# Opening loads reordered in a two-layer hybrid token mixer, with early modulation weights in other buffers

## The chip, the cores and the metric

One core of a Trainium2 chip runs the whole program. The metric is the device time of one execution in microseconds (us). TensorE (PE) multiplies matrices, VectorE (DVE), ScalarE (ACT) and GpSimd (POOL) work on tiles, SyncE (SP) issues most DMAs. An engine executes its instructions in the order in which they were put on it; the engines wait for one another through semaphores.

## The reference, cut to what matters

Two layers work on two streams of 256 tokens each, width 1024: stream 0 is the context, stream 1 the latent. What the change touches is the head of the first layer: modulation vectors from `c` and `c_ctx`, the modulated norm of both streams, and the first input projection (the low-rank latents `mla_cq`, `mla_ckv`, `mla_kr` and `gla_glr`, 448 columns in all).

```python
shift, scale, gate = jnp.split(jax.nn.silu(c) @ ada_w[l] + ada_b[l], 3, axis=-1)
shift_c, scale_c, gate_c = jnp.split(jax.nn.silu(c_ctx) @ ada_w[l] + ada_b[l], 3, axis=-1)
h = rms_norm(x, pre_g[l]) * (1.0 + scale[:, None]) + shift[:, None]
hc = rms_norm(cx, pre_g[l]) * (1.0 + scale_c) + shift_c
...
cq = rms_norm(in_proj(hh, w_in, 'mla_cq'), q_norm)
```

Behind that each layer runs four mixers (latent attention, neighbourhood attention, long convolution, gated linear attention), gates and merges them, and projects the sum; all of that is the same in both kernels.

## The kernel before, in words

Everything is f32; a product is made of three matmuls, because each operand is split into a high part (a rounded copy, made on ScalarE) and a low part (the difference, made on VectorE). Weights come as `raw` tiles of 448 or 512 KB (`piece`, L422, three buffers) and leave as pairs `wh`, `wl` from a pool of eight each.

Work is written as generators. `spawn` (L300) enters a task, `drive` (L308) keeps a clock that advances by estimated matmul costs and lets the task of best priority that is ready run its next piece; the pauses come from the table `WAIT` (L207) and, for the first modulation, from `ADA_AT` (L204). What comes out of this is TensorE's order, which is fixed. The other engines and the DMA queue get their order from a scheduler that works on the written program.

The head of the program, in `main` (L1516): rows of x go to four tiles `x0` (512 KB each; two for stream 0, two for stream 1), then come the modulation weights of layer 0 for scale and shift. They are eight pieces of 1 MB: quarter `j` of the channels (0 to 3) times `part` (shift, scale), each loaded by `ada_load` (L543) in two halves. Quarters 0 and 1 go to `wh`/`wl` buffers (all 16 of them), quarter 2 to the pool `s`, quarter 3 to the four `x0` buffers once these are free. Between them stand the four pieces of the latent weights (`w_latent`, 448 KB each).

`ada_first` (L582) takes the eight pieces in turn: 16 small matmuls into a PSUM tile `ada`, a copy of it (`rows`) by VectorE, four matmuls that turn it by 90 degrees (`adat`, in `ada_sum` L559), and an addition into `ab`, the scale and shift per channel. `norm_in` (L629), one task per stream, squares the rows on ScalarE, gets the reciprocal root on GpSimd (`rstd`), scales on VectorE (`xn`), turns them on TensorE in four quarters (`ht`), applies scale and shift (`h`, one half on VectorE, then the other on ScalarE) and splits the result into `hh` and `hl`. `ht` and `adat` share two PSUM buffers (pool `pt`). `latent_in` (L879) multiplies: per block of 128 tokens and quarter six matmuls `pa`. Quarter q of it wants `ab` of quarter q and the q-th piece of latent weights.

`filters` (L711) makes the long convolution's filters beside this; its tiles `w3h`, `w3l` come from the pool `gy` (tags `gh`, `gl`, four each), and GpSimd clears part of `w3l`. `setup_rest` loads small tables.

Of the kernel before, what the change touches and what calls it, by code (L numbers as in the profile page):

```python
# [9 lines left out]
F32 = mybir.dt.float32  # L10
# [6 lines left out]
P = 128  # L17
# [108 lines left out]
def _layout(x, c, ctx, c_ctx, ada_w, ada_b, pre_g, post_g, w_in, mla_q_norm, mla_w_uq, mla_kv_norm, mla_w_ukv, na_rpb,  # L126
# [74 lines left out]
PI_C3 = float(np.float32(TWO_PI - PI_C1 - PI_C2))  # L201
PI_MAX = 3.1415925
MAGIC = 12582912.0
ADA_AT = (6.0, 8.0, 6.0, 11.0, 15.0, 17.0, 17.5, 19.5)  # L204


WAIT = {  # L207
    "ada_sum": (1.34, 0),
    "ada_load": (7.75, 9.57),
    "ada_gap": (4.19, 8.22),  # L210
# [47 lines left out]
    "merged": (4.6, 3.55),  # L258
    "merged_step": (0.48, 0),
    "merged_out": (1.6, 1.24),  # L260
    "norm_first": (2.15, 8.0),
}


# [5 lines left out]
class Block:  # L270
# [63 lines left out]
    def wait(self, name):  # L334
        return WAIT[name][self.l]

# [245 lines left out]
    def ada_first(self, pieces):  # L582
        for j in range(4):
            yield 0
            for part in range(2):
                yield max(0.0, ADA_AT[2 * j + part] - self.clock)
                ps = self.ps(self.pa, "ada")
                for half in range(2):
                    self.ada_mm(half, pieces[j, part, half], ps, half == 0, half == 1)
                rows = self.ada_rows(part)  # L590
                self.nc.vector.tensor_copy(rows, ps[:, 0:256])
                yield self.wait("ada_sum")
                self.ada_sum(0, part, j, rows)
            self.abq[0] = j + 1
# [818 lines left out]
    def layer(self, l, ws):  # L1413
# [12 lines left out]
        else:  # L1426
            halves = {c: self.rows(self.w_latent(l, (2 * c, 2 * c + 1))) for c in (1, 0)}
            ws = halves.get
        for g in ((0, 1),) if l == 0 else ((1,), (0,)):
            a = self.spawn(self.latent_in(l, ws, g, outs, lats), 0)  # L1430
            if g[0] in outs:
                yield lambda: a.done
# [83 lines left out]
    def main(self):  # L1516
        nc, d = self.nc, self.d
        self.setup()
        self.h, self.ht, self.hq, self.abq, self.aq = {}, {}, [0, 0], [0, 0], 0
        loaded = [self.filter_mlp(0)]  # L1520
        self.load_first()
        pieces = {}

        def ada(j, alloc):
            for part in range(2):
                for half in range(2):
                    pieces[j, part, half] = self.ada_load(0, part, j, half, alloc(half))

        early = lambda half: [self.wp.tile([P, 512], F32, tag=("wh", "wl")[half], name=self.name("adaw")) for _ in range(2)]
        xt = {}  # L1530
        for s in range(2):
            for j in range(2):
                xt[s, j] = self.M("x0")
                nc.sync.dma_start(xt[s, j], d["xin"][2 * s : 2 * s + 2, :, j * 512 : j * 512 + 512].rearrange("t p n -> p t n"))
        ada(0, early)
        ada(1, early)
        first = self.w_latent(0, (0, 1))
        ada(2, lambda half: [self.S("adaw"), self.S("adaw")])
        first += self.w_latent(0, (2, 3))
        ada(3, lambda half: [self.M("adaw").rearrange("p a b -> p (a b)")])  # L1540
        loaded += [self.window(self.S), self.filter_in(0, 0)]
        nc.sync.dma_start(self.dft, d["dft"])
        loaded.append(self.filter_in(0, 1))

        def later():
            yield from self.ada_first(pieces)
            self.setup_rest()

        self.spawn(later(), 0)
        for s in range(2):  # L1550
            self.spawn(self.norm_in(0, s, [xt[s, 0], xt[s, 1]]), 0)
        self.filt_task = self.spawn(self.filters(0, loaded), 1)

        def layers():
            for l in range(DEPTH):
                yield from self.layer(l, first if l == 0 else None)

        self.spawn(layers(), 5)
        with self.tc.manual_schedule(engines={mybir.EngineType.PE}):
            self.drive()  # L1560
# [19 lines left out]
```

## Time and profile before

| | |
|---|---|
| median of 3 runs | 1393.2 us (1391.38 to 1393.54) |
| the profiled execution | 1392.82 us |
| its span, first to last instruction | 1391.0 us |
| TensorE busy | 1310.1 us, 94% of the span |
| VectorE, ScalarE, GpSimd busy | 901.3, 603.4, 320.2 us |
| read from HBM | 163.45 MB, 122 GB/s over the span |

Times below are counted from the span's start. A busy engine is one with an instruction in it; matmuls overlap, so a busy TensorE need not be at its peak. Idle time of an engine stands in brackets with what ended it.

### The profile page before, as it was taken

The numbers are of one execution on the slowest core, as the hardware profiler recorded it, in microseconds if no ns is written. First come the engines' busy times: TensorE is split into PE (matmuls) and PEld (weight loads), VectorE is DVE, ScalarE is ACT, GpSimd is POOL, SyncE is SP. The second block draws the span as 40 slices with busy tenths as digits, with TensorE's granted clock in tenths as the row PEclk, the third lists the DMA queues.
The fourth block names the chain that finished last, engine by engine and source line by source line (L and its number), as shares of the span: only waits on it lengthen the run. The fifth ranks groups of instructions, "written<-read, shape, count | busy, mean of one in ns | idle before, by whom it ended". The sixth has DMA issues, their size and how long they took to land.

```text
span 1391.0 us, 20163 instructions
## 1 busy us (share of the span) xinstructions
PE 1310.1 (94%) x7444; PEld 1033.3 (74%) x7444; DVE 901.3 (65%) x1676; ACT 603.4 (43%) x1268; POOL 320.2 (23%) x408
## 2 busy tenths in 40 slices
PE   5899999989999999999999999979996999999996
PEld 3767677767777687666767777778775889788875
DVE  4678754676443446656565687977577787768764
ACT  4455553432322233222244454465556456445452
POOL 2232201233320201113301122442113431122110
PEclk9999999999999999999999999999998999999999
DMA  9521213232233433332422353433152366535362
GB/s 342 184 91 53 100 46 101 91 118 91 93 121 137 137 106 117 113 119 93 144 84 90 105 153 110 147 100 116 34 163 88 103 198 211 165 95 181 107 206 67
DMA packets 55506, 171.07 MB, mean 123 GB/s; under 512 B 7470, under 2 KB 10128, under 8 KB 55408
## 3 DMA queue, kind: packets, MB, share of 16 engines
q1 hardware_dynamic: 49056, 153.31, 33.4%
q0 software_dynamic: 5440, 16.16, 3.6%
q8 instruction: 59, 0.97, 0.3%
q10 hardware_dynamic: 912, 0.31, 0.1%
q14 instruction: 39, 0.32, 0.1%
HBM read 163.45 MB, written 6.31 MB: 122 GB/s over the span
## 4 chain that ended last, share of the span: by engine, by line
PE 40%; DVE 7%; issue 3%; ACT 3%; DMA 2%; POOL 1%; DVEq 0%; POOLq 0%; ACTq 0%
PE pc L386 11%; PE pj L386 10%; PE br L386 5%; PE wo L386 3%; PE sc L386 2%; PE y L386 2%; DVE wl L376 2%; PE pt L400 2%; DMA raw<-in_w_out 1%; PE pa L386 1%; ACT wh L435 1%; PE yc L386 1%; DMA raw<-in_w_in 1%; DVE ub L370 0%; PE go L386 0%
## 5 line engine op out<-in xcount | busy, mean ns | idle before, releaser
L376 DVE TENSOR_TENSOR wl<-raw,wh 128x512 fp32r<-128x512 f32 (+1 forms) x416 | 305.5, 756 | 178.2 <-ACT wh L435 171.4
L435 ACT CAST wh<-raw 128x512 fp32r<-128x512 f32 (+1 forms) x416 | 248.9, 618 | 279.9 <-DMA raw<-in_w_in 145.3
L386 PE MATMUL pc<-hh,wh 128*128 128x256 f32 (+1 forms) x688 | 242.4, 352 | 7.4 <-DVE cv L379 3.4
L386 PE MATMUL pc<-hl,wh 128*128 128x256 f32 (+1 forms) x688 | 231.5, 337 | 0.0
L386 PE MATMUL pc<-hh,wl 128*128 128x256 f32 (+1 forms) x688 | 231.3, 336 | 0.0
L386 PE MATMUL pj<-wh,hh 128*128 128x512 f32 x512 | 212.8, 416 | 3.1 <-DVE zg L379 1.6
L386 PE MATMUL pj<-wl,hh 128*128 128x512 f32 x512 | 200.2, 391 | 0.4 <-DVE wl L376 0.4
L386 PE MATMUL pj<-wh,hl 128*128 128x512 f32 x512 | 200.2, 391 | 0.0
L386 PEld LDWEIGHTS pc<-hh,wh 128*128 128x128 f32 x688 | 132.2, 192 | 32.8 <-issue 15.0
L386 PEld LDWEIGHTS pc<-hl,wh 128*128 128x128 f32 x688 | 132.2, 192 | 14.3 <-issue 2.6
L386 PEld LDWEIGHTS pc<-hh,wl 128*128 128x128 f32 x688 | 132.0, 192 | 13.7
L386 PEld LDWEIGHTS pj<-wh,hh 128*128 128x128 f32 x512 | 96.2, 188 | 33.3 <-issue 12.0
L386 PEld LDWEIGHTS pj<-wh,hl 128*128 128x128 f32 x512 | 96.1, 188 | 21.1
L386 PEld LDWEIGHTS pj<-wl,hh 128*128 128x128 f32 x512 | 96.5, 188 | 20.2 <-issue 2.6
L376 POOL TENSOR_TENSOR gl<-y,gh 128x256 fp32r<-128x256 f32 (+1 forms) x44 | 36.2, 830 | 293.5 <-ACT gh L418 293.5
L822 ACT ACTIVATE p<-sc,mx 128x512 f32<-128x512 f32 (+1 forms) x96 | 59.0, 616 | 59.3 <-DVE mx L820 56.0
L386 PE MATMUL br<-wh,gh 128*128 128x512 f32 x192 | 79.1, 412 | 5.0 <-DVE merged L379 2.6
L386 PE MATMUL br<-wl,gh 128*128 128x512 f32 x192 | 76.7, 399 | 0.0
L386 PE MATMUL br<-wh,gl 128*128 128x512 f32 x192 | 76.4, 398 | 0.0
L1336 ACT ACTIVATE gt<-pj 128x512 f32<-128x512 f32 x48 | 28.6, 596 | 90.0 <-PE pj L386 87.5
L820 DVE TENSOR_REDUCE mx<-sc 128x1 f32<-128x512 f32 (+1 forms) x96 | 55.1, 592 | 11.4 <-PE sc L386 10.5
L837 ACT COPY pt<-pt 128x256 f32<-128x256 f32 x96 | 34.2, 373 | 43.1 <-PE pt L400 42.1
(287 smaller groups left out, 2223.6 us busy)
## 6 DMA issues: line engine op xcount, KB each, us to landing
raw<-in_w_in SPq DMA_DIRECT2D x160, 512.0 KB, 3.6
adaw<-in_ada_w SPq DMA_DIRECT2D x36, 512.0 KB, 3.6
raw<-in_w_branch SPq DMA_DIRECT2D x32, 512.0 KB, 3.6
raw<-in_w_out SPq DMA_DIRECT2D x16, 512.0 KB, 4.3
adaw<-in_ada_w SPq DMA_DIRECT2D x24, 256.0 KB, 6.1
H<-filt POOLq DMA_DIRECT2D x16, 256.0 KB, 4.0
nab<-in_na_bias POOLq DMA_DIRECT2D x16, 256.0 KB, 3.0
raw<-in_w_in SPq DMA_DIRECT2D x8, 448.0 KB, 4.9
```

The source lines that it names most:

```text
L376: eng.tensor_tensor(out=out, in0=a, in1=b, op=ALU.subtract)
L386: self.nc.tensor.matmul(out, lhsT, rhs, start=start, stop=stop, skip_group_check=skip)
L400: self.nc.tensor.transpose(out, in_, self.ident)
L435: nc.scalar.copy(hi, raw[:, sl])
L820: nc.vector.tensor_reduce(out=mx, in_=ps[h][:, :nk], axis=AX.X, op=ALU.max, negate=True)
L822: nc.scalar.activation(p[h][:, :nk], ps[h][:, :nk], AF.Exp, bias=mx, scale=1.0, accum_out=sm)
L837: nc.scalar.copy(pts[h][b // 2], pp[:, b : b + 2, :])
L1336: self.nc.scalar.activation(gates[s, t], ps, AF.Tanh, scale=0.5)
```

## The change

The order of the opening loads becomes: rows of stream 1, quarter 0 of the modulation weights, two pieces of latent weights, rows of stream 0, quarters 1 and 2, the other two latent pieces, quarter 3. Quarter 0 goes to the pool `gt`, quarter 1 to the pool `gy`, so that `wh`/`wl` hold none of it. The norm of stream 1 is entered before that of stream 0, `latent_in` takes stream 1 first, and `norm_first` is longer. The table `ADA_AT` moves into `WAIT` with the same numbers.

```diff
@@ -201,10 +201,14 @@
 PI_C3 = float(np.float32(TWO_PI - PI_C1 - PI_C2))
 PI_MAX = 3.1415925
 MAGIC = 12582912.0
-ADA_AT = (6.0, 8.0, 6.0, 11.0, 15.0, 17.0, 17.5, 19.5)
+
 
 
 WAIT = {
+    "ada_at0": (6.0, 8.0),
+    "ada_at1": (6.0, 11.0),
+    "ada_at2": (15.0, 17.0),
+    "ada_at3": (17.5, 19.5),
     "ada_sum": (1.34, 0),
     "ada_load": (7.75, 9.57),
     "ada_gap": (4.19, 8.22),
@@ -258,7 +262,7 @@
     "merged": (4.6, 3.55),
     "merged_step": (0.48, 0),
     "merged_out": (1.6, 1.24),
-    "norm_first": (2.15, 8.0),
+    "norm_first": (3.27, 8.0),
 }
 
 
@@ -583,7 +587,7 @@
         for j in range(4):
             yield 0
             for part in range(2):
-                yield max(0.0, ADA_AT[2 * j + part] - self.clock)
+                yield max(0.0, WAIT[f"ada_at{j}"][part] - self.clock)
                 ps = self.ps(self.pa, "ada")
                 for half in range(2):
                     self.ada_mm(half, pieces[j, part, half], ps, half == 0, half == 1)
@@ -1426,7 +1430,7 @@
         else:
             halves = {c: self.rows(self.w_latent(l, (2 * c, 2 * c + 1))) for c in (1, 0)}
             ws = halves.get
-        for g in ((0, 1),) if l == 0 else ((1,), (0,)):
+        for g in ((1, 0),) if l == 0 else ((1,), (0,)):
             a = self.spawn(self.latent_in(l, ws, g, outs, lats), 0)
             if g[0] in outs:
                 yield lambda: a.done
@@ -1526,15 +1530,18 @@
                 for half in range(2):
                     pieces[j, part, half] = self.ada_load(0, part, j, half, alloc(half))
 
-        early = lambda half: [self.wp.tile([P, 512], F32, tag=("wh", "wl")[half], name=self.name("adaw")) for _ in range(2)]
         xt = {}
-        for s in range(2):
+
+        def rows_of(s):
             for j in range(2):
                 xt[s, j] = self.M("x0")
                 nc.sync.dma_start(xt[s, j], d["xin"][2 * s : 2 * s + 2, :, j * 512 : j * 512 + 512].rearrange("t p n -> p t n"))
-        ada(0, early)
-        ada(1, early)
+
+        rows_of(1)
+        ada(0, lambda half: [self.G("adaw"), self.G("adaw")])
         first = self.w_latent(0, (0, 1))
+        rows_of(0)
+        ada(1, lambda half: [self.F("adaw", tag="gh"), self.F("adaw", tag="gl")])
         ada(2, lambda half: [self.S("adaw"), self.S("adaw")])
         first += self.w_latent(0, (2, 3))
         ada(3, lambda half: [self.M("adaw").rearrange("p a b -> p (a b)")])
@@ -1547,7 +1554,7 @@
             self.setup_rest()
 
         self.spawn(later(), 0)
-        for s in range(2):
+        for s in (1, 0):
             self.spawn(self.norm_in(0, s, [xt[s, 0], xt[s, 1]]), 0)
         self.filt_task = self.spawn(self.filters(0, loaded), 1)
```

The queue of SyncE, its first loads (`x` rows, `adaw` modulation weights, `raw` latent weights; the rows left out are more `adaw`). Before:

```order
L1534 DMA x_2_129<-in_xin 128x2x512
L1534 DMA x_3_131<-in_xin 128x2x512
L1534 DMA x_4_133<-in_xin 128x2x512
L1534 DMA x_5_135<-in_xin 128x2x512
L548 DMA adaw_137<-in_ada_w 128x512
...
L426 DMA raw_169<-in_w_in 128x896
L426 DMA raw_179<-in_w_in 128x896
```

The change:

```order
L1538 DMA x_2_129<-in_xin 128x2x512
L1538 DMA x_3_131<-in_xin 128x2x512
L552 DMA adaw_133<-in_ada_w 128x512
...
L430 DMA raw_149<-in_w_in 128x896
L430 DMA raw_159<-in_w_in 128x896
L1538 DMA x_22_169<-in_xin 128x2x512
L1538 DMA x_23_171<-in_xin 128x2x512
```

Sixteen `adaw` loads stand ahead of the first `raw` before, eight in the change, and the second pair of `x` has gone behind both `raw`.

VectorE around the fifth piece of modulation (`rows_123` is its copy; `h32` the modulated rows, `ht` their turned source, `wl` low parts of latent weights). Before:

```order
L379 SCALAR_TENSOR_TENSOR ab0_99<-ab0_99,par0_122 128x2x2
L591 COPY rows_123_442<-ada_122_433 128x256
L383 TENSOR_SCALAR h32_125_455<-ht_124_450,ab0_99 128x256
L383 TENSOR_SCALAR h32_129_475<-ht_120_417,ab0_99 128x256
L373 TENSOR_TENSOR ab0_99<-adat_126_460,par0_122 128x2x2
```

The change:

```order
L383 SCALAR_TENSOR_TENSOR ab0_99<-ab0_99,par0_122 128x2x2
L387 TENSOR_SCALAR h32_124_450<-ht_120_417,ab0_99 128x256
L595 COPY rows_123_442<-ada_122_433 128x256
L380 TENSOR_TENSOR wl_42_208<-raw_40_205,wh_41_207 128x448
L380 TENSOR_TENSOR wl_44_212<-raw_40_205,wh_43_211 128x448
L387 TENSOR_SCALAR h32_126_460<-ht_125_455,ab0_99 128x256
L380 TENSOR_TENSOR wl_47_218<-raw_45_215,wh_46_217 128x448
L377 TENSOR_TENSOR ab0_99<-adat_127_465,par0_122 128x2x2
```

The older `ht` (ht_120) is read ahead of the copy and of the younger one, where before it was read behind both; `wl` of the later latent pieces now stand in between.

GpSimd, the four reciprocal roots (`rstd`) of the first norms and the clearing of `w3l`. Before:

```order
L738 MEMSET w3l_131_481 64x512
L738 MEMSET w3l_133_486 64x512
...
L407 TENSOR_TENSOR rstd_92_296<-ms_91_295,mhalf_103 128x1
L407 TENSOR_TENSOR rstd_97_307<-ms_96_306,mhalf_103 128x1
```

The change:

```order
L411 TENSOR_TENSOR rstd_95_309<-ms_94_308,mhalf_103 128x1
L742 MEMSET w3l_132_486 64x512
L742 MEMSET w3l_134_491 64x512
L411 TENSOR_TENSOR rstd_100_320<-ms_99_319,mhalf_103 128x1
```

The two MEMSETs, at the head of the queue before, stand between the third and the fourth root.

## Rows read from the trace of the kernel before

**Rows 1.** engine totals of the page: busy us, share of the span, instructions

```profile
PE 1310.1 (94%) x7444; PEld 1033.3 (74%) x7444; DVE 901.3 (65%) x1676; ACT 603.4 (43%) x1268; POOL 320.2 (23%) x408
```

**Rows 2.** busy time by stretch of the span (columns in the first line)

```profile
core 0: us, PE busy (x) PEld busy (x) DVE busy (x) ACT busy (x) POOL busy (x), PEclk, DMA share, GB/s
0.00:47.00 47.00, 29.82 (x202) 17.50 (x202) 22.62 (x63) 19.25 (x43) 7.98 (x18) 1.00 0.95 350
...
34.00:46.00 12.00, 9.10 (x85) 6.31 (x84) 6.39 (x16) 4.21 (x9) 0.00 (x0) 1.00 1.02 401
...
65.30:82.00 16.70, 13.94 (x71) 11.59 (x70) 15.36 (x33) 10.98 (x31) 9.32 (x13) 0.98 0.36 111
```

**Rows 3.** TensorE in order of time, first 66 us: start, us, work [idle before <-releaser]

```profile
18.92 1.93 PE L386 MATMUL ada<-adaw,sv 128*32 128x256 f32 x16
...
24.74 1.11 PE L400 MATMUL ht<-ident,xn 128*128 128x128 f32 x4
27.74 1.01 PE L386 MATMUL adat<-par,rows 128*128 128x2 f32 x4 [1.89 <-ACT h L662]
28.68 1.93 PE L386 MATMUL ada<-adaw,sv 128*32 128x256 f32 x16
30.55 1.11 PE L400 MATMUL ht<-ident,xn 128*128 128x128 f32 x4
...
34.01 1.07 PE L386 MATMUL ada<-adaw,sv 128*32 128x256 f32 x16
...
38.17 0.61 PE L386 MATMUL adat<-par,rows 128*128 128x2 f32 x4 [1.24 <-ACT h L662]
...
40.80 0.61 PE L386 MATMUL adat<-par,rows 128*128 128x2 f32 x4 [0.43 <-DVE rows L591]
41.33 1.07 PE L386 MATMUL ada<-adaw,sv 128*32 128x256 f32 x16
...
45.49 0.61 PE L386 MATMUL adat<-par,rows 128*128 128x2 f32 x4 [1.24 <-ACT h L662]
46.03 1.07 PE L386 MATMUL ada<-adaw,sv 128*32 128x256 f32 x16
...
51.41 0.65 PE L400 MATMUL ht<-ident,xn 128*128 128x128 f32 x4 [0.81 <-DVE ab L373]
...
65.29 0.39 PE L386 MATMUL f<-w3h,a 128*128 128x512 f32 x1
```

**Rows 4.** VectorE in order of time, same columns

```profile
36.98 1.00 DVE L383 TENSOR_SCALAR h<-ht,ab 128x256 f32<-128x256 f32 x2 [1.40 <-PE ht L400]
...
47.51 3.77 DVE L376 TENSOR_TENSOR wl<-raw,wh 128x448 fp32r<-128x448 f32 x4
```

**Rows 5.** ScalarE in order of time, same columns

```profile
7.78 0.63 ACT L639 ACTIVATE xn<-x 128x512 f32<-128x512 f32 x1 [3.25 <-DMA pos<-in_w]
...
12.08 0.61 ACT L639 ACTIVATE xn<-x 128x512 f32<-128x512 f32 x1
...
24.34 2.07 ACT L435 CAST wh<-raw 128x448 fp32r<-128x448 f32 x4 [7.10 <-DMA raw<-in_w_in]
...
37.55 1.02 ACT L662 ACTIVATE h<-ht,ab 128x256 f32<-128x256 f32 x2 [4.91 <-DVE h L383]
```

**Rows 6.** GpSimd in order of time, same columns

```profile
1.27 0.98 POOL L738 MEMSET w3l<- 64x512 f32 x2
```

**Rows 7.** DMA of the first 60 us: GB/s in 40 slices of 1.5 us

```profile
GB/s 0 121 352 356 250 396 355 373 292 279 242 321 392 410 416 415 404 407 407 415 428 418 401 410 407 422 391 418 396 417 242 23 11 25 268 161 238 8 55 284
```

**Rows 8.** DMA issues on SyncE in order of time

```profile
37.69 0.33 SPq L426 DMA_DIRECT2D raw<-in_w_in  x1
```

**Rows 9.** TensorE behind the first projections, at 80 us

```profile
80.47 0.32 PE L400 MATMUL glrp<-ident,kr 128*96 128x128 f32 x1 [2.76 <-DVE glrT L376]
```

**Rows 10.** the start of the second layer, TensorE and then VectorE

```profile
919.50 0.53 PE L386 MATMUL pa<-wh,hl 128*128 128x192 f32 x1 [1.52 <-DVE hl L376]
...
918.76 0.68 DVE L376 TENSOR_TENSOR hl<-h,hh 128x512 fp32r<-128x512 f32 x1
```

## The prediction

> **What bounds the kernel now.** I read the engine totals first, then the stretches of the span, then the first 66 us engine by engine. TensorE is busy for 94% of the span [rows 1], so the kernel is nearly one long row of matmuls, and a change of loads can only win where TensorE still waits. It does so in the head: up to 47 us it is busy for 29.8 us, VectorE for 22.6 us, while the DMA engines are 95% busy at 350 GB/s [rows 2]. It would be easy to call the head bound by DMA. The timeline speaks against that. Of the waits shown for TensorE between 24 us and 52 us none ends with a DMA [rows 3]: 1.89 us and twice 1.24 us on ScalarE's `h`, 0.43 us on the copy `rows`, 0.81 us on `ab`. From there to 65.29 us, the first `f`, it runs on `pa` without a wait of note.
>
> How early could the data be there? I add up the GB/s of [rows 7] to megabytes against time. Before, the two first latent pieces end at 7.4 MB (x 2.1, small tables 0.24, sixteen `adaw` of 0.262, two pieces of 0.459); the first of them alone at 7.0 MB, which is passed at 22.9 us. ScalarE's first `wh` starts at 24.34 us, having waited for it [rows 5], so I take 1.4 us from that sum to use. The last modulation piece of before ends at 12.1 MB, 35.3 us, is usable at 36.7 us and is multiplied at 46.03 us [rows 3]: 9 us late. The chain of small steps through two PSUM buffers sets the head, not the bytes.
>
> **The change part by part.** The same bytes move; only their order, their buffers and the order of the streams differ. TensorE does the same matmuls and turns, in a slightly other order, all within the head.
>
> *Loads.* By the same sum, plus 1.4 us: quarter 0 is usable at 13.7 us, the two latent pieces at 17.0 us, stream 0's rows at 20.3 us, quarter 1 at 22.9 and 25.4 us, quarter 2 at 28.0 and 30.5 us, the later latent pieces at 31.6 and 32.7 us, quarter 3 at 35.2 and, behind window and `w3`, 40.3 us. Before, the fourth latent piece was issued at 37.69 us, behind filter loads [rows 8].
>
> *The first stage, to the start of the fourth piece of modulation.* Before, that piece starts at 28.68 us, after `ht` at 24.74 us, a wait and `adat` [rows 3]; the wait is ScalarE's `h`, which came late because four `wh` casts, from 24.34 us on, and their `wl` stood on ScalarE and VectorE just then [rows 5]. In the change the casts are due at 17 us, before that hour. New in their place: stream 0's rows land at 20.3 us; then three more squares at 0.61 us (eight took 7.78 to 12.69 us [rows 5]) end at 22.3 us; VectorE does `xn`, `h`, two filter steps and the copy `rows` in between, in all some 2.7 us; so the last `xn`, for which `ht` waits, ends at about 25.5 us. The second `w3l` MEMSET, 0.98 us for both at 1.27 us before and beside nothing [rows 6], now waits for the third piece (about 23.4 us) with the fourth root behind it; it ends at 24.4 us and costs at most some tenths. Then the last two turns 0.5 us and `adat` 1.0 us at the slow pace: 27.0 us, or 26.4 us where the copies fit in earlier. I take 26.4 us: **2.3 us** earlier. Bounds: 25.0 us, if quarter 1 sets it with no queue before it (3.7 us), and 28.0 us, if all VectorE steps stand in line (0.7 us).
>
> *Fourth to fifth piece.* 28.68 to 34.01 us before [rows 3], without a wait; the same work: 0.
>
> The lag of 1.4 us has a page against it. The Trainium skill, "DMA: Bandwidth & Descriptors", section "Anatomy of one DMA", gives a nearly constant cost of some 2 us per transfer, most of it the receipt of the last byte ahead of the semaphore. By that the rows of stream 0 come 0.6 us later, the gain of this stage would be 1.7 us, and the time 1388.6 us, an estimate. The case's own 24.34 us stands nearer, and I stay with it.
>
> *Fifth piece to the run of `pa`.* The waits from 34.01 us on are 1.24, 0.43, 1.24 and 0.81 us, 3.72 us in all [rows 3]. The first has its cause in VectorE's order: the `h` of two `ht` are done together at 36.98 us, after a wait of 1.40 us for the younger one, ScalarE's two follow at 37.55 us [rows 4, 5], and `adat` wants the older one's buffer. The change's VectorE takes the older `h` directly after `ab`. The second 1.24 us has the same form and goes the same way. The 0.81 us is `ab` standing behind four `wl` that took 3.77 us [rows 4]; two of those are of the fourth latent piece and are now done ten microseconds earlier. What is late next: four `wl` between fifth and sixth piece, some 2.4 us, delay the copy `rows` there; I keep 1.2 us of waits. So **2.5 us** gained; bounds 1.2 us and 3.7 us (none, all). The eighth piece would start at about 41.2 us, its data are there at 40.3 us: cover, by 0.9 us.
>
> *Buffers.* `gt` and `gy` are not used so early, and `wh`/`wl` are free for the latent casts at once; 0 beside what is counted, since the casts then wait for data alone. Stream 1 first in `latent_in`: same matmuls, 0. The renamed table: 0.
>
> *Second layer's start.* The scheduler also moves some VectorE steps there, a `hl` ahead of a `wl`; TensorE waited 1.52 us for the last `hl` [rows 10]. It can win that or lose about as much on the `hl` that moved back: counted 0, bounds 1.5 us on each side.
>
> Sum: 1392.82 (the profiled execution, 0.4 us under the median of 1393.2 us) − 2.3 − 2.5 = **1388.0 us**.
>
> **The rivals.**
>
> *Quarter 3 becomes the bound.* It goes behind 1 MB of filter loads. If the rate stays at 346 GB/s, about what 4.5 to 24 us showed on the mean, instead of 401 GB/s [rows 2, 7], the last 8.3 MB behind stream 0's rows take 23.9 us from 18.9 us, and the last piece is usable at 44.2 us, 3.0 us after TensorE wants it: gain 1.8, time 1391.0 us. For: the early slices. Against: 18 slices at 391 to 428 GB/s.
>
> *The gain is taken back at 80 us.* There TensorE waits 2.76 us for VectorE [rows 9], which is busy 15.4 of 16.7 us [rows 2]. If VectorE's row there began no earlier, all but some half microsecond would be lost: 1392.3 us. Against: what starts it, the latents' results and weight buffers, is released by TensorE.
>
> *Slower: the rows of stream 0 come late.* VectorE and ScalarE run in order, and stream 1's first `h` stands behind the first `xn` of stream 0 on both. The fourth piece follows these rows by 26.4 − 20.3 = 6.1 us. They decide from 25.1 us on: then that piece starts at 31.2 us, 2.5 us later than before, and the saved waits are used up. At 28 us, +2.9 us: 1395.7 us. For: a pair of loads only follows when earlier ones have landed, and the lowest slice is 242 GB/s [rows 7]. Against: even at 242 GB/s throughout from 1.5 us on, their 5.35 MB are there at 23.6 us and usable at 25.0 us.
>
> *Slower: TensorE stays at its low clock.* Sixteen `ada` matmuls took 1.93 us at 18.92 and 28.68 us, 1.07 us from 34.01 us on [rows 3]: about the ratio of 1.2 to 2.4 GHz, though the granted clock reads 1.00 throughout [rows 2]. TensorE had no gap from 28.68 us until then. If the change leaves gaps and the low level lasts to the eighth piece, the 9.1 busy us of 34 to 46 us [rows 2] grow by some 7: 1395.0 us. Against: the change closes gaps there.
>
> The Trainium skill says the same against this change ("TensorE: Matmul & The Clock Gate", section "HAM oscillation"): waits on loads between groups of matmuls can drop the clock, so that each group starts slow. The trace before shows it at low level through its waits up to 28.68 us, and at high level through waits of 1.24 us.
>
> **How the numbers follow.** Forecast 0.70, quarter 3 late 0.08, taken back 0.12, late rows 0.05, low clock 0.05. The forecast's bounds add up to 1392.82 − 3.7 − 3.7 − 1.5 = 1383.9 us and 1392.82 − 0.7 − 1.2 + 1.5 = 1392.4 us; the lowest needs all three at once, so I begin at 1384.4. The range 1384.4 to 1392.5 us then takes in the first two rivals and leaves out the slow ones, 0.10, and little of the forecast. A measurement here can tell some 0.2%, 2.8 us, from no change. Faster by more: nearly all of the forecast, 0.68. Slower by more: 0.10. The rest 0.22.
>
> **What would show it.** Right: the fourth piece of `ada` starts near 26.4 us and the eighth near 41.2 us, the first `f` near 60.5 us, `adat` no longer waits 1.24 us for ScalarE's `h`, and the shift of nearly 5 us is still there at 110 us and at the end. Wrong: a wait of TensorE on `adaw` at the eighth piece (quarter 3), an idle VectorE ahead of stream 0's `xn` beyond 23 us (late rows), `ada` groups of 1.93 us beyond 34 us (clock), or a wait at 80 us grown by as much as the head has won.

## The result, and the profile after

| | before | changed |
|---|---|---|
| median, 5 runs each on one chip | 1391.51 us (1388.78 to 1393.54) | 1384.55 us (1382.79 to 1385.38) |
| ratio, 95% interval | | 0.9946 [0.9931, 0.9962] |
| the profiled execution, its span | 1392.82, 1391.0 us | 1384.55, 1382.8 us |
| first `f` | 65.29 us | 60.04 us |
| the `glrp` that waits at 80 us | 80.47 us | 74.85 us |

A second set of 12 runs gave 0.9948 [0.9930, 0.9966]. The change is faster, clear of noise, by some 7.4 us or 0.5%; I had forecast 4.8 us. Lines of the changed kernel stand 4 higher than in the rows of before.

TensorE in order of time in the changed kernel (start, us, work, [idle before <-releaser]), against [rows 3]:

```profile
12.85 2.56 PE L390 MATMUL ada<-adaw,sv 128*32 128x256 f32 x16
...
19.79 2.98 PE L390 MATMUL ada<-adaw,sv 128*32 128x256 f32 x16 [0.46 <-DMA adaw<-in_ada_w]
22.70 0.48 PE L404 MATMUL ht<-ident,xn 128*128 128x128 f32 x1
25.73 0.90 PE L404 MATMUL ht<-ident,xn 128*128 128x128 f32 x3 [2.56 <-DVE xn L387]
26.43 0.85 PE L390 MATMUL adat<-par,rows 128*128 128x2 f32 x4
27.21 1.93 PE L390 MATMUL ada<-adaw,sv 128*32 128x256 f32 x16
...
32.40 1.07 PE L390 MATMUL ada<-adaw,sv 128*32 128x256 f32 x16
...
38.13 0.58 PE L390 MATMUL adat<-par,rows 128*128 128x2 f32 x4 [0.87 <-DVE rows L595]
...
41.83 1.07 PE L390 MATMUL ada<-adaw,sv 128*32 128x256 f32 x16
...
60.04 0.39 PE L390 MATMUL f<-w3h,a 128*128 128x512 f32 x1
```

The reader sees three things. The waits of `adat` for ScalarE's `h` are gone; from the fifth piece on 0.87 us on `rows` is what is left of 3.72 us. The fourth piece starts only 1.47 us earlier (28.68 to 27.21), behind a new wait of 2.56 us for VectorE's last `xn`. And up to there the groups still run at the low level, 1.93 us for sixteen matmuls.

Behind that new wait, VectorE and GpSimd:

```profile
20.97 0.88 DVE L387 TENSOR_SCALAR xn<-x,rstd 128x512 f32<-128x512 f32 x2
...
24.20 1.87 DVE L387 TENSOR_SCALAR xn<-x,rstd 128x512 f32<-128x512 f32 x2 [0.44 <-POOL rstd L411]
```

```profile
21.63 0.68 POOL L742 MEMSET w3l<- 64x512 f32 x1 [0.69 <-PE ada L390]
22.84 0.52 POOL L742 MEMSET w3l<- 64x512 f32 x1 [0.53 <-PE ada L390]
23.44 0.73 POOL L411 TENSOR_TENSOR rstd<-ms,mhalf 128x1 f32<-128x1 f32 x1
24.14 1.26 POOL L380 TENSOR_TENSOR hl<-h,hh 128x512 fp32r<-128x512 f32 x1
```

The clearing of `w3l`, which stood beside nothing at 1.27 us before [rows 6], now waits for the third piece to leave `gy`, with the root for the last `xn` behind it; and two `xn` that take 0.88 us alone take 1.87 us beside GpSimd's `hl`.

The windows, of before [rows 2] and of the changed kernel: up to 47 us TensorE is busy for 34.69 us instead of 29.82.

```profile
0.00:47.00 47.00, 34.69 (x228) 21.52 (x229) 26.35 (x70) 22.03 (x46) 9.96 (x19) 1.00 0.97 361
```

At 75 us and at the start of the second layer, against [rows 9] and [rows 10]:

```profile
74.85 0.31 PE L404 MATMUL glrp<-ident,kr 128*96 128x128 f32 x1 [2.20 <-DVE glrT L380]
...
909.31 0.36 PE L390 MATMUL pa<-wh,hl 128*128 128x192 f32 x1 [0.64 <-DVE hl L380]
911.56 0.36 PE L390 MATMUL pa<-wh,hl 128*128 128x192 f32 x1 [0.66 <-POOL hl L380]
```

### The profile page after: what moved, and what is told of

Its sections match the earlier page's. It is cut to its first block, busy times and chain, and to the rows that moved or that the text cites. A ratio compares the mean times of both kernels' runs of the same rounds, so it can differ in the third digit from the quotient of the medians.

```text
span 1382.8 us, 20166 instructions
## 1 busy us (share of the span) xinstructions
PE 1311.0 (95%) x7444; PEld 1033.8 (75%) x7444; DVE 898.5 (65%) x1676; ACT 604.2 (44%) x1268; POOL 319.1 (23%) x408
## 4 chain that ended last, share of the span: by engine, by line
PE 42%; DVE 7%; issue 3%; ACT 2%; DMA 2%; POOL 1%; DVEq 0%; POOLq 0%; ACTq 0%
PE pc L390 12%; PE pj L390 11%; PE br L390 5%; PE wo L390 3%; PE sc L390 2%; PE y L390 2%; PE pt L404 2%; DVE wl L380 2%; PE pa L390 1%; PE yc L390 1%; ACT wh L439 1%; DMA raw<-in_w_out 1%; DMA raw<-in_w_in 1%; DVE ub L374 0%; DVE wr L380 0%
## 5 line engine op out<-in xcount | busy, mean ns | idle before, releaser
L380 DVE TENSOR_TENSOR wl<-raw,wh 128x512 fp32r<-128x512 f32 (+1 forms) x416 | 300.3, 744 | 178.1 <-ACT wh L439 175.8
L390 PEld LDWEIGHTS pj<-wl,hh 128*128 128x128 f32 x512 | 96.6, 189 | 20.3 <-issue 2.6
L826 ACT ACTIVATE p<-sc,mx 128x512 f32<-128x512 f32 (+1 forms) x96 | 58.9, 615 | 59.4 <-DVE mx L824 56.2
L824 DVE TENSOR_REDUCE mx<-sc 128x1 f32<-128x512 f32 (+1 forms) x96 | 55.0, 591 | 11.4 <-PE sc L390 10.5
```

The source lines that it names most:

```text
L380: eng.tensor_tensor(out=out, in0=a, in1=b, op=ALU.subtract)
L390: self.nc.tensor.matmul(out, lhsT, rhs, start=start, stop=stop, skip_group_check=skip)
L824: nc.vector.tensor_reduce(out=mx, in_=ps[h][:, :nk], axis=AX.X, op=ALU.max, negate=True)
L826: nc.scalar.activation(p[h][:, :nk], ps[h][:, :nk], AF.Exp, bias=mx, scale=1.0, accum_out=sm)
```

## The experiments

The times and places of all runs, for the sections below (before: median 1391.6 us over 78 runs; the start of `f` and of the waiting `glrp` are from each kernel's profile):

| run | what it is | first `f` | `glrp` | ratio to before |
|---|---|---|---|---|
| e1 | before again | 65.5 | 80.7 | 1.0008 [0.9995, 1.0022] |
| e2 | changed kernel again | 60.7 | 75.5 | 0.9948 [0.9930, 0.9966] |
| e3 | before, new buffers alone | 64.3 | 79.5 | 1.0006 [0.9994, 1.0018] |
| e4 | changed, old buffers | 60.2 | 75.0 | 0.9960 [0.9946, 0.9974] |
| e5 | before, streams alone | 55.0 | 71.8 | 0.9935 [0.9912, 0.9958] |
| e12 | e5 again | 55.6 | 72.5 | 0.9944 [0.9924, 0.9964] |
| e9 | before, norm order alone | 57.3 | 73.1 | 0.9951 [0.9935, 0.9967] |
| e10 | before, latent order alone | 63.8 | 78.6 | 0.9996 [0.9981, 1.0011] |
| e11 | changed loads, old streams | 72.7 | 87.7 | 1.0057 [1.0038, 1.0077] |
| e6 | changed, stream 0's rows earlier | 58.6 | 74.1 | 0.9935 [0.9911, 0.9958] |
| e7 | changed, quarter 1 in `s` | 58.9 | 73.7 | 0.9923 [0.9900, 0.9946] |
| e8 | changed, filler in the gap | 58.4 | 73.2 | 0.9918 [0.9895, 0.9941] |
| e13 | changed, latents behind quarter 1 | 58.1 | 73.7 | 0.9944 [0.9931, 0.9958] |
| e14 | e7 and e8 together | 57.7 | 72.6 | 0.9922 [0.9905, 0.9938] |

### The same programs again

> The kernel of before, unchanged, for the spread of one and the same program. Both theories: the first f starts at 65.3 us within 0.3 us, as in [rows 3], and the ratio is 1.000 within 0.002. Theory A (the change is worth 5.3 us in the head, about 0.6 us at 80 us and some 1 us at the second layer's start; what else two profiles show between them is the place of the intervals at granted clock 0.5): those intervals stand elsewhere than in the first profile, and instruction starts of the two profiles of the same program drift apart by 2 to 4 us in places behind 480 us. Theory B (a gain of 8 us that is all the change's, part of it in later waits): they stay within 1 us of each other.

> The changed kernel, unchanged. Theory A: first f at 60.0 us within 0.3 us, shift against before 5.0 to 5.6 us at 66 to 480 us and 6 to 7 us on the mean behind 930 us, ratio 0.9950 within 0.0012 (6.9 us under before). Theory B: the shift at the end is 8 us or more again, ratio 0.994 or less.

Two profiles of before agree within 1 us up to 250 us and then drift apart, by some 3 us in one direction at 700 to 800 us and by 2.1 us in the other at the end. The granted clock drops to 0.5 for short stretches, in seven to eleven places of an execution and not always the same. So a difference of a few us between two profiles behind 480 us cannot be laid to the change by itself, and theory B falls; of the 9 us that the first two profiles showed at 930 us, only part can be kept. The changed kernel's second profile has its first `f` at 60.74 us, 0.4 us beyond what I had expected: against e1 the shift there is 4.8 us, not 5.25.

### The buffers

e3 puts quarters 0 and 1 of before into the new buffers, e4 puts those of the changed kernel back:

```diff
-        ada(0, early)
-        ada(1, early)
+        ada(0, lambda half: [self.G("adaw"), self.G("adaw")])
+        ada(1, lambda half: [self.F("adaw", tag="gh"), self.F("adaw", tag="gl")])
```

> Before with the first two groups of modulation weights in gt and gy, all loads, streams and orders as before. Theory A (the order of loads counts): four wh casts wait for raw, which lands where it did, so the first cast still starts at 24.3 us within 0.5 us, the first f at 65.0 to 65.5 us, ratio 1.000 within 0.001. Rival (the buffers wh and wl held the casts back, and freeing them is what wins): the first f at 62.5 us or earlier, ratio 0.998 or less.

> The changed kernel with the first two groups of modulation weights back in wh and wl. Theory A: quarter 0 has been multiplied or loaded early enough that the four casts are held back by at most 1 us, first f at 60.0 to 60.8 us, same time as the changed kernel within 0.1 per cent (ratio to before 0.995 to 0.996). Rival (buffers count): casts wait for the third piece of modulation and the latents are late by 3 us or more, first f at 63 us or later, ratio 0.997 or more.

Both times say that buffers count for nothing that can be measured here. In e3 the casts began at 23.3 us and the first `f` came at 64.3 us, 0.5 and 0.7 us under what I had expected. In e4 a cost did show, where I had not looked: the third piece (quarter 1) waits 6.97 us for its weights and starts at 24.72 us. Its loads want the `wh`/`wl` buffers that the first two pieces leave, and stand behind quarter 2 in SyncE's queue. Yet the first `f` is at 60.2 us, for then the fourth piece is already at the high level:

```profile
24.72 2.96 PE L390 MATMUL ada<-adaw,sv 128*32 128x256 f32 x16 [6.97 <-DMA adaw<-in_ada_w]
...
29.30 1.07 PE L390 MATMUL ada<-adaw,sv 128*32 128x256 f32 x16
```

### Loads or streams

The run that overturned my reading. e5 keeps all loads of weights as before and only takes stream 1 first (rows, norm, latents):

```diff
-        for g in ((0, 1),) if l == 0 else ((1,), (0,)):
+        for g in ((1, 0),) if l == 0 else ((1,), (0,)):
...
-        for s in range(2):
+        for s in (1, 0):
             for j in range(2):
                 xt[s, j] = self.M("x0")
...
-        for s in range(2):
+        for s in (1, 0):
             self.spawn(self.norm_in(0, s, [xt[s, 0], xt[s, 1]]), 0)
```

> Before with the rows of stream 1 loaded first, its norm entered first and the latents multiplied for stream 1 first; modulation weights and latent weights are loaded as before and stand in the buffers of before. Theory A (the order of the loads wins, the order of the streams counts nothing by itself): the first wh cast stays at 23.3 to 24.3 us, the first f starts at 64.5 to 66.0 us, ratio 1.000 within 0.0015. Rival (half of the gain is the order of the streams, which lets ab and h of the waiting stream go first): first f at 62.5 us or earlier, ratio 0.998 or less.

The rival held, and by more than it had asked: first `f` at 55.0 us, 5 us before the changed kernel's. TensorE in e5:

```profile
19.30 1.52 PE L386 MATMUL ada<-adaw,sv 128*32 128x256 f32 x16
20.75 0.66 PE L400 MATMUL ht<-ident,xn 128*128 128x128 f32 x4
22.25 0.58 PE L386 MATMUL adat<-par,rows 128*128 128x2 f32 x4 [0.85 <-DVE rows L591]
22.76 1.07 PE L386 MATMUL ada<-adaw,sv 128*32 128x256 f32 x16
...
36.82 1.07 PE L386 MATMUL ada<-adaw,sv 128*32 128x256 f32 x16
...
55.03 0.39 PE L386 MATMUL f<-w3h,a 128*128 128x512 f32 x1
```

The latent weights arrive no earlier than before (the casts start at 23.9 us), and the fourth piece still starts at 22.76 us instead of 28.68. From this I formed theory C. TensorE turns stream 1's first `ht` ahead of stream 0's in both kernels. Before, VectorE has the `h` of the two in the other order:

```order
L383 TENSOR_SCALAR h32_115_392<-ht_114_387,ab0_99 128x256
L383 TENSOR_SCALAR h32_116_397<-ht_103_336,ab0_99 128x256
```

`ht_103_336` is the older one, in its PSUM buffer since 15.67 us; its `h` could run as soon as `ab` is there, but stands behind the `h` of `ht_114_387`, which TensorE turns at 24.74 us. Theory C as I wrote it down says that the next `adat` wants the older one's buffer. The rows of before say that it takes the younger one's:

```profile
26.55 0.99 DVE L383 TENSOR_SCALAR h<-ht,ab 128x256 f32<-128x256 f32 x2
```

```profile
27.12 1.02 ACT L662 ACTIVATE h<-ht,ab 128x256 f32<-128x256 f32 x2
```

ScalarE's two `h` run from 27.12 to 28.14 us in that same order, and `adat` starts at 27.74 us, when the first of them, the younger tile's, has ended and the second has not. At 38.17 us it is the same (`h` from 37.55 to 38.57 us), and at 45.49 us (44.88 to 45.90 us); the buffers of the written program agree. So what `adat` waits through is a chain: turn, VectorE's `h`, ScalarE's `h` of the tile just turned, since the older tile still holds the other buffer. With the older `h` first, the older tile's buffer is empty long before, and `adat` takes that one. The remedy of theory C is the same either way. Four runs test it. e9 turns round one line, the second `for s` above; e10 the first line alone; e11 takes the changed kernel's loads and buffers and puts the streams back; e12 repeats e5.

> Before with one line changed: the norm of stream 1 is entered ahead of that of stream 0; loads, buffers and the order in which the latents are multiplied stay. Theory C, formed from the run with the streams alone (first f at 55.0 us instead of 65.3 with the loads of before): before, VectorE and ScalarE take the h of the younger ht first and the older one's behind it, and adat wants the older one's PSUM buffer, once per quarter; entering stream 1 first turns that round. Then no adat waits for ScalarE's h, the first f starts at 55 to 58.5 us, ratio 0.9925 to 0.995. Rival D (what counted there is that the rows of stream 1 land first, or that the latents begin with stream 1): first f at 63 us or later, ratio 0.998 or more.

> Before with only the order in which the latents are multiplied turned round, stream 1 first. Theory C: nothing, first f at 65.0 to 66.0 us, ratio 1.000 within 0.0015. Rival D: first f at 62 us or earlier, ratio 0.998 or less.

> The changed kernel's loads and buffers with the streams as before (norm of stream 0 entered first, latents with stream 0 first, norm_first 2.15). Theory C (the load order gives nothing by itself and needs the order of the streams): VectorE takes stream 0's xn first, whose rows land at 19 us, and TensorE's first ht wants stream 1's behind them; so the second piece of modulation starts at 24 to 27 us instead of 18.9, the first f at 67 to 73 us, ratio 1.001 to 1.006. The theory of my forecast (earlier latents win 2.3 us in the first stage): first f at 63 us or earlier, ratio 0.998 or less.

> The streams alone once more, as in the first such run, for its time and for whether TensorE's level is the program's or chance: there the granted clock's record began at 14.0 us and ada groups took 1.07 us from 22.8 us on; before, and in the changed kernel, they took 1.93 us until 28.7 and 27.2 us. If the order sets it (TensorE has fewer gaps ahead of 22 us): the level is high again by 16 us and the first f starts at 54.5 to 55.8 us. If chance: low groups up to 27 us or later, first f at 57 to 60 us. Ratio 0.9925 to 0.9950 in the first case.

e9 gives as much as the whole change, with one line: 0.9951, first `f` at 57.3 us, and VectorE's `h` of the older `ht` at 21.61 us, right behind `ab`, instead of second in a pair from 26.55 us on:

```profile
21.15 0.16 DVE L379 SCALAR_TENSOR_TENSOR ab<-ab,par 128x4 f32<-128x4 f32 x1
21.27 0.43 DVE L379 SCALAR_TENSOR_TENSOR argr<-arg 128x256 f32<-128x256 f32 x1
21.61 0.54 DVE L383 TENSOR_SCALAR h<-ht,ab 128x256 f32<-128x256 f32 x1
...
23.79 0.55 DVE L383 TENSOR_SCALAR h<-ht,ab 128x256 f32<-128x256 f32 x1 [0.31 <-PE ht L400]
```

`adat` follows its `ht` without a wait. But the one line does a second thing, which theory C leaves out. Before, VectorE does stream 0's `xn` first while TensorE turns stream 1's first, so TensorE waits early as well; in e9 it does not. Before, then e9:

```profile
15.67 0.48 PE L400 MATMUL ht<-ident,xn 128*128 128x128 f32 x1 [1.40 <-DVE xn L383]
17.45 0.90 PE L400 MATMUL ht<-ident,xn 128*128 128x128 f32 x3 [1.30 <-DVE xn L383]
```

```profile
13.94 1.12 PE L400 MATMUL ht<-ident,xn 128*128 128x128 f32 x4
...
20.77 1.93 PE L386 MATMUL ada<-adaw,sv 128*32 128x256 f32 x16
...
23.54 0.87 PE L386 MATMUL adat<-par,rows 128*128 128x2 f32 x4
24.34 1.93 PE L386 MATMUL ada<-adaw,sv 128*32 128x256 f32 x16
```

The third piece, at 22.88 us before, is 2.1 us earlier by this, of 8.0 us that e9 wins up to the first `f`. No run parts the two. `norm_first` was not turned by itself; e5 and e9 have the old value.

e10 does nothing to the time (0.9996; its first `f` came 1.2 us earlier than expected, at 63.8 us, with the fourth piece at 1.18 us instead of 1.93). e11 is slower than before by 8 us, with every wait for `h` still there:

```profile
24.78 0.48 PE L404 MATMUL ht<-ident,xn 128*128 128x128 f32 x1 [13.58 <-DVE xn L387]
26.52 0.90 PE L404 MATMUL ht<-ident,xn 128*128 128x128 f32 x3 [1.26 <-DVE xn L387]
28.00 1.93 PE L390 MATMUL ada<-adaw,sv 128*32 128x256 f32 x16
...
37.20 0.61 PE L390 MATMUL adat<-par,rows 128*128 128x2 f32 x4 [2.27 <-ACT h L666]
```

VectorE works off stream 0's `xn` first there, whose rows now land last, while TensorE asks for stream 1's: 13.58 us of wait. The wait of 2.27 us at 37.20 us is no clean test of the casts, for the later latent pieces' casts and `wl` (31.20 to 36.1 us) stand ahead of the `h` there. The load order alone is a loss, and the order of the norms is what makes it bearable and what wins.

### What the load order costs beside the streams

e12 agrees with e5: first `f` at 55.6 us, high level again by 22 us, so the early head is most likely the program's and not chance. The first granted-clock entry of the trace stands at 14.0 and 15.0 us in e5 and e12, at 33.4 us before and 31.7 us in the changed kernel. The changed kernel's first `f` is 5 us later than theirs. Three parts of the changed kernel's loads were turned back one at a time, and the gap was filled (e8). The rows of stream 0 ahead of the latents:

```diff
-        first = self.w_latent(0, (0, 1))
         rows_of(0)
+        first = self.w_latent(0, (0, 1))
```

> The changed kernel with the rows of stream 0 loaded ahead of the first two latent pieces. Theory A (what sets the start of the fourth piece, 27.2 us, is the last xn of stream 0, for which ht waits 2.56 us): xn is ready some 2.5 us earlier, the wait goes, the fourth piece starts at 24.8 to 25.5 us and the first f at 58.2 to 59.2 us; ratio to before 0.9935 to 0.9945. Rival (the head is bounded by TensorE's low level up to 32 us and by quarter 3 behind it, whichever way the first stage goes): first f at 59.7 us or later, ratio as the changed kernel, 0.995.

Quarter 1 in another pool, out of GpSimd's way:

```diff
-        ada(1, lambda half: [self.F("adaw", tag="gh"), self.F("adaw", tag="gl")])
+        ada(1, lambda half: [self.S("adaw"), self.S("adaw")])
```

> The changed kernel with quarter 1 of the modulation weights in the pool s instead of gy; TensorE's order is the same. In the changed kernel GpSimd's second w3l clearing waits for the third piece of modulation to leave gy and ends at 23.4 us, and the reciprocal root for the last xn stands behind it. Theory A: the root comes at 22.4 to 22.8 us, the last xn and the fourth piece 0.6 to 1.0 us earlier, the first f at 59.0 to 59.6 us, ratio to before lower than the changed kernel's by 0.0005, which this measurement can hardly tell. Rival (the last xn is slow because GpSimd's hl runs beside it: two xn took 1.87 us beside it and 0.88 us without): root earlier, but xn no shorter, and fourth piece earlier by less than 0.4 us unless xn ends before hl begins.

e6: the 2.56 us wait is gone, the fourth piece starts at 25.90 us, 0.4 us later than expected, and the first `f` at 58.6 us as expected. e7: the root comes at 22.87 us instead of 23.44 and the wait shrinks to 0.85 us; the fourth piece starts at 25.71 us, 1.5 us earlier where I had expected 0.6 to 1.0, and the first `f` comes at 58.9 us (59.0 to 59.6 expected). In e7 the second of the two `xn` still runs beside `hl`, and the pair takes 1.89 us; both readings had a part.

> The changed kernel with five extra matmuls (128x256, results never read) on TensorE in the 2.56 us in which ht waits for the last xn. Theory A (low level costs time in the head: 16 ada matmuls took 1.93 us at 27.2 us and 1.07 us from 32.4 us on): with the gap filled TensorE goes up to the high level before the fourth piece, that piece takes 1.07 us, and the fifth starts at 30.0 to 31.0 us instead of 32.4; quarter 3, which lands near 40 us, keeps the eighth from coming before 40 us, so the first f is at 58.2 to 59.2 us, ratio to before 0.9935 to 0.9945. Rival (the filler gives nothing back since VectorE and data set the pace): fifth piece at 32 us or later, first f at 60 us or later.

The filler, in `norm_in`, between the turns of the two `xn`:

```diff
+                    if l == 0 and s == 0 and kt == 0 and i == 1:
+                        for _ in range(5):
+                            self.mm(ps[:, 1, :], self.ident, xn[0][0][:, 0:256], cost=0)
...
```

```profile
23.64 2.51 PE L390 MATMUL ht<-xn,ident 128*128 128x256 f32 x10
26.23 0.55 PE L404 MATMUL ht<-ident,xn 128*128 128x128 f32 x3
...
27.06 1.07 PE L390 MATMUL ada<-adaw,sv 128*32 128x256 f32 x16
...
30.96 1.07 PE L390 MATMUL ada<-adaw,sv 128*32 128x256 f32 x16
```

The x10 are the five matmuls, two records each. The fourth piece starts where it did, and takes 1.07 us; the fifth starts 1.44 us earlier; the ratio, 0.9918, lies under the 0.9935 to 0.9945 that I had expected. Work that computes nothing wins time here, since it takes the place of a gap: the granted clock is back at 1.00 from 24 us on, and in e7, which has no filler, not before 31 us. e14, with the same filler, shows it again: its fourth piece, at 26.83 us, takes 1.07 us. One caution: e7, e8 and e14 ran at the high level from some 10.5 to 17.5 us already, which the profiles of the changed kernel do not show, though e8 is the same program up to the filler. So that early stretch is not the program's alone, and how much it helped is not known. Busy time by stretch, columns as in [rows 2], of e8 and then of e7:

```profile
17.50:23.50 6.00, 3.07 (x17) 0.88 (x18) 4.89 (x16) 3.65 (x11) 1.07 (x2) 0.50 1.05 400
24.10:31.00 6.90, 6.12 (x51) 4.77 (x51) 3.59 (x8) 2.29 (x5) 2.76 (x3) 1.00 1.05 412
```

```profile
18.00:31.00 13.00, 10.19 (x52) 6.16 (x53) 8.21 (x22) 5.75 (x14) 3.72 (x4) 0.50 1.05 408
32.00:40.00 8.00, 7.37 (x74) 5.27 (x67) 6.36 (x15) 5.11 (x11) 0.00 (x0) 1.00 1.04 411
```

Then the latents behind quarter 1 (e13), and e7 and e8 together (e14):

```diff
-        first = self.w_latent(0, (0, 1))
         rows_of(0)
         ada(1, lambda half: [self.F("adaw", tag="gh"), self.F("adaw", tag="gl")])
+        first = self.w_latent(0, (0, 1))
```

> The changed kernel with the first two latent pieces loaded behind quarter 1 instead of ahead of stream 0's rows; TensorE's order is that of the changed kernel. Theory C1 (latents ahead of quarter 1 starve the third and fourth piece of modulation, which leaves TensorE gaps and its low level): the third piece starts at 18.5 to 20 us without the 2.56 us wait for the last xn behind it, the fourth at 22.3 to 24.5 us, the latents are cast by 23 us, the first f starts at 54.5 to 57.5 us as with the streams alone, the glrp that waits for VectorE at 71.5 to 73.5 us (74.85 in the changed kernel); ratio 0.992 to 0.995. Rival C2 (the loss lies in the buffers or in norm_first): first f at 59 us or later.

> The changed kernel with quarter 1 in the pool s and the five unread matmuls ahead of the last xn's turn. Single runs gave a first f at 58.9 and 58.4 us instead of 60.0. Theory C: the root and the last xn come 0.7 us or more earlier, so five fillers of some 0.45 us may now end behind xn and cost up to 1 us; first f at 57.5 to 58.8 us, glrp at 72.5 to 73.5 us, ratio 0.991 to 0.9945. Rival (what is won ahead of 75 us is lost again behind it): ratio as the changed kernel, 0.9948, or more.

e13 brings the third piece to 18.79 us and the fourth to 23.64 us as C1 said, but both and part of the fifth still run at the low level (1.93, 1.93 and 1.71 us), and the first `f` comes at 58.1 us, over C1's 57.5 and under C2's 59: the order of the loads explains some 2 of the 5 us. The rest stands beside groups at the low level; that the level is its cause is not shown. Why e5 keeps the high level from 22 us on and e13 does not is left open. Its `glrp` at 73.7 us is 0.2 us beyond what C1 allowed. e7, e8 and e14 have the lowest times, 0.9923, 0.9918 and 0.9922, against 0.9946 and 0.9948 for the changed kernel, so putting the two edits together adds nothing that can be measured. The intervals still touch; that any of the three beats the changed kernel is likely, not shown. Each beats before clearly.

## Why the prediction was right or wrong

**The first stage: right in sign, wrong in cause.** I had the fourth piece 2.3 us earlier because the latents' casts would no longer stand in front of `h` when `adat` waits. It was 1.47 us, and mostly not for that: e9 moves the piece to 24.34 us with the casts where they were (24.83 us). The step that failed is the sentence that the wait of 1.89 us at 27.74 us comes from the casts. The same chain, the turn and both `h` of the tile just turned, costs 1.24 us in each later round, where no casts stand. So the casts and their `wl` account for 0.65 us at most: VectorE's `h` could have started when `ht` ended at 25.85 us and began at 26.55 us, behind this `wl`:

```profile
26.02 0.62 DVE L376 TENSOR_TENSOR wl<-raw,wh 128x448 fp32r<-128x448 f32 x1
```

I saw the mechanism in the second half of the head and did not look whether it stood in the first.

**The buffer was the wrong one.** For the later rounds I wrote that `adat` wants the older tile's buffer; it waits for the younger one's (the two `h` of before, under Loads or streams). That the waits go when the older `h` runs first was right all the same, because that frees the older buffer for `adat`. The conclusion was right for a reason other than mine, and in that part I was lucky.

**The order of the norms had no term.** "Same matmuls, 0" was said of the latents, and is right (e10). For the order in which the norms are entered I had no term, and it gives by itself what the whole change gives (e9). I had read VectorE's new order as something that comes with the change as a package, and never asked which edit brought it. Nor did I look ahead of 24 us, where before has 2.70 us of waits for `xn`.

**The last `xn`.** I had it end at 25.5 us. The data were not late: the casts began at 15.45 us, where I had said 17.0 for both pieces, and the second half of stream 0's rows was in use at 19.10 us, where I had said 20.3. It ended at 26.07 us, mainly because the two `xn` took 1.87 us instead of 0.88, a term I did not have. The second clearing ahead of their root I had priced at "some tenths", and it cost 0.57 us (the root at 23.44 us, against 22.87 in e7). The lag of 1.4 us was too long: by the DMA record of the changed kernel the bytes up to these loads had moved 1.0 to 1.1 us ahead of their use. The Trainium skill's 2 us ("DMA: Bandwidth & Descriptors", section "Anatomy of one DMA") stands there for transfers that GpSimd issues; these are SyncE's. By the sum of bytes with it the rows come at 20.9 us, an estimate, and they were in use at 17.8 and 19.1 us.

**Fourth to fifth piece, 0.** 5.19 us instead of 5.33: right.

**From the fifth piece on.** 2.5 us forecast; measured from there to the first `f` 31.28 us before and 27.64 after, 3.64 us: 2.85 us of waits (3.72 to 0.87) and 0.79 us less busy time for the same work, a term I did not have. The 2.5 us was the term most under its size.

**The eighth piece** starts at 41.83 us (41.2 forecast), the first `f` at 60.04 us (60.5). Quarter 3 did not bind; the piece begins without a wait.

**80 us and the second layer.** The gain was not taken back: 5.25 us at the first `f`, 5.62 us at `glrp` (4.8 and 5.2 us by e1 and e2). At the second layer's start I had counted 0 with 1.5 us on each side. From the first `pa` of that stage to its last `lat` the changed kernel takes 44.65 us (885.85 to 930.50), and two kernels with before's order there and as much time at the low granted clock take 45.40 us (e9) and 45.58 us (e3): 0.8 to 0.9 us won. Where that stage has twice as much low time, before and e13 take 47.22 and 47.24 us and e7 and e8, with the changed order, 45.75 and 45.82 us: 1.4 to 1.5 us. No edit is aimed at this; it comes from where the scheduler put some `hl`.

**The sum.** 1.47 us at the fourth piece (2.3 forecast), 0.14 to the fifth (0), 3.64 to the first `f` (2.5), 0.37 to `glrp` (0) and 0.8 to 1.5 us at the second layer (0) make 6.4 to 7.1 us, where 4.8 was forecast. The rest to 7.4 us lies within the intervals. The time of 1388.0 us missed by more than the gain did, since I began the sum at one execution, 1392.82 us, and the median of before over all runs is 1391.6 us. The 12 runs of e2 also show a higher mean granted clock than those of before (0.982 against 0.980), and over all runs a time falls by some 0.4 us per 0.001 of it (a fit); whether the change brings that is not shown.

**The clock rival** was right about the place and wrong about the sign of the whole: the changed kernel keeps gaps, two short ones on loads (0.43 us at 10.31 us and 0.46 us) and a new one of 2.56 us on VectorE's `xn`, and stays at the low level to 32 us. e8 shows what the last one costs, 1.4 us at the fifth piece. Waits on loads with a falling clock behind them stand in e7 and e8:

```profile
19.96 3.01 PE L390 MATMUL ada<-adaw,sv 128*32 128x256 f32 x16 [2.37 <-DMA adaw<-in_ada_w]
```

```profile
20.43 3.02 PE L390 MATMUL ada<-adaw,sv 128*32 128x256 f32 x16 [3.35 <-DMA adaw<-in_ada_w]
```

The granted clock falls to 0.5 in these waits, at 17.7 and 17.2 us, and stays there to 31 us in e7 and to 24 us in e8, which has the filler. The Trainium skill's warning ("TensorE: Matmul & The Clock Gate", section "HAM oscillation"), that waits on loads between groups of matmuls can drop the clock, so that each group starts slow, agrees with these two rows. In the changed kernel the low level cost part of the gain, not all of it.

## What to carry to other kernels

When several steps share two buffers, find out which buffer the next step takes; here it is the one whose readers were written first. Where that is the tile just filled, the next step waits through that tile's whole chain each time round, and no load order mends it. A release by an engine shows which tile it was only when the times are compared: the step that starts halfway through a pair of `h` waited for the first of the pair. When a change has several edits, price each by itself, the one that "only reorders" above all: here one line of entering two tasks was worth 7 us, and the reordered loads without it cost 8. A wait that the trace names once in each round has one cause first, and only what goes beyond its common size (1.89 against 1.24 us) needs another.

## What the runs showed of the hardware that was not expected

Some VectorE instructions slow beside GpSimd. In the changed kernel 14 `xn` took 468 to 546 ns; the two that ran beside 1.2 us of GpSimd work took 1478 and 1507 ns (at 24.20 and 863.10 us). A 0.28 us `argr` took 1.35 us in e4, at 23.85 us, beside an `hl` on GpSimd from 23.55 to 25.05 us. Each of the slow ones began after the GpSimd instruction and ended 0.15 to 0.3 us behind its end. Not all are slowed: an `xn` that began in e4 at 23.45 us, 0.1 us ahead of that `hl`, took 479 ns, and before, the copy `rows` at 30.68 us took 0.42 us beside an `hl`.

The granted clock of a window reads 1.00 from 0 to 47 us before and in the changed kernel, while sixteen `ada` matmuls take 1.93 us early in that stretch and 1.07 us later, about the ratio of 1.2 to 2.4 GHz. The level there is to be read from the durations.
